# Branch A's norm factors spread through memory and multiplied on GpSimd; token sums converted in three buffers

## The chip, the cores and the metric

The kernel runs on one core of one Trainium2 chip. The metric is the time of one execution on the device in microseconds, the median of several runs. A core has five engines with an instruction queue each: TensorE (PE in the profile, with its weight loads as PEld), VectorE (DVE), ScalarE (ACT), GpSimd (POOL) and SyncE (SP), which here issues nearly all DMAs. Each engine runs its queue in order, and waits on semaphores for what other engines or DMAs must have done first.

## The reference, cut to what matters

A bidirectional encoder block in float32: 16 meta tokens and 1024 tokens of width 1024. The tokens are normed and projected; branch A (differential attention, 4 heads of 128 values, no window) and branch B (windowed attention, 8 heads) run side by side; each branch is projected and gated by a sigmoid; the sum goes through the output projection, and a SwiGLU layer and a final norm follow. The part that the change touches is the norm of branch A's heads:

```python
attn = jax.nn.softmax(s1, axis=-1) - lam * jax.nn.softmax(s2, axis=-1)
y = jnp.einsum('bhqk,bkhe->bqhe', attn, v)
...
y = rms_norm(y, subln_g) * (1.0 - lambda_init)   # per token and head, over the 128 values
...
merged = jax.nn.sigmoid(ga) * (y_a @ w_ba) + jax.nn.sigmoid(gb) * (y_b @ w_bb)
```

## The kernel before

Every float32 product is made from a high and a low part of each operand (`split`, L124: ScalarE writes the high part at L125, another engine the low part at L126), so one product is three matmuls. The gates, the projections behind the branches and the feed-forward layer use a scheme with seven products of half-size blocks in place of eight, whose operands are sums and differences of blocks.

The program runs in four stretches: norm, transposes and first projections (to about 95 us in the profile); branch B's attention with the projections of branch A (95 to 285); branch A's attention with the two gates' projections (285 to 600); the rest (600 to 1400).

**Branch B.** `attend_b` makes, for each of two groups and eight tiles of queries, scores (L417), exponentials on ScalarE (L423, with the small sink term `bes` at L425), a denominator on VectorE (L426, L427), transposes on TensorE (bpt, L458) that VectorE or ScalarE copies to SBUF (btr, L461 and L462), and products with the values (bpy). Between these stand projection matmuls (L237). Order: a scheduler with a model of the engines places the instructions of this stretch. In the same stretch `tokens_mixed` (L338 to L367) forms the sums and differences of token blocks on GpSimd that the gates' products need later. Each is split by `kept` into a tile `tst`, high part on ScalarE (L125), low part on GpSimd (L126), and stored by SyncE into `t_d`. Two buffers of the pool `kvpool` (tags q1 and q0) take turns: a split waits until the store from two splits earlier has landed.

**Branch A.** 32 tiles of queries (head h = 0 to 3, tile t = 0 to 7), one after the other. TensorE's order is written by hand: for each tile a string of `SLOTS` is read letter by letter; `s` is a step of the tile's scores (`aps`, L1054), `t` a step of transposes of the tile before (`apt`, L1084), `g` a quarter of a gate's operand group, 12 matmuls with one weight operand `wopg` (L943), `n` a step of the tail (products with the values, L1097, and the norm, `normed_a`). Heads 0 and 1 take two strings in turn, heads 2 and 3 a third one and, for every fourth tile, `SLOTS_3`. GpSimd makes the gate operands (L820 to L840: sums of weight blocks, a cast `wopg` L839, the low part L840), copies far parts of the bias mask (L1006, `far_copy`), zeroes ends of value tiles (L1026) and takes the power −1/2 (L1116). Its order here is left to the scheduler, with some ordering edges: `queue_behind(late, first)` (L373) puts an instruction behind another one in the schedule without a semaphore. SyncE loads gate weights (`wg`, L799), keys, values and token sums (`hT`, from `t_d`, L869) and stores results.

**The norm** (`normed_a`, once for each of eight groups of four tiles, (h, c) with c = 0 or 1). Head outputs stand transposed: 128 values on partitions, 512 tokens along the row. ScalarE writes the squares into `ysq` and the values times the gain into `yg`; four small matmuls with a column of ones (L1110) give the sums of squares with tokens on partitions, four columns of 128; VectorE and GpSimd turn them into the factors `f` (tile `af`, 128×4; L1114 to L1116). `N_WAIT` = 3 tail steps later four transposes of `f`, each column broadcast to 128 columns, give in a PSUM bank (`apf`, L1121) each token's factor on all 128 partitions; VectorE multiplies `yg` by that bank (L1122), and SyncE stores `yg` into `ya_d` (L1123).

Of the kernel before, what the change touches and what calls it, by code (L numbers as in the profile page):

```python
# [9 lines left out]
F32 = mybir.dt.float32  # L10
F32R = mybir.dt.float32r
# [8 lines left out]
P = 128  # L20
# [23 lines left out]
FAR_LATE = 6  # L44
LAST_B = ("T1", 4), (5, "V0"), (5, "T2"), ("T2", 6), (7, "V1"), (7, "V2")
SLOTS_LAST = "ggggntgntnt"
SLOTS_3 = "ssgsgngsstsgntgnt"
S_BUFS = (2, 2)
AT_BUFS = 2
G_BUFS = 3  # L50
# [29 lines left out]
def encoder_block(ctx: ExitStack, tc: tile.TileContext, x, meta, norm_mix, w_in, lq1, lk1, lq2, lk2,  # L80
# [254 lines left out]

    HALF = (slice(0, 512), slice(512, S))

    def tokens_mixed():  # L338
# [659 lines left out]
    s0s = [apool.tile([P, 9 * P], F32, name=f"as0_{i}") for i in range(2)]  # L998
    apool.tile([P, 9, 2, 256], F32R, tag="at", name="at_room", bufs=AT_BUFS)

    def far_copy(n):
        if n < AH * NT:
            with ExitStack() as after:
                if n > 2:
                    after.enter_context(tc.issue_after(made_g[-1].ins))
                nc.gpsimd.tensor_copy(far_m[n % 3][:, 0:S - 704], dist[:, 1600 - n % NT * P:1600 - n % NT * P + S - 704])  # L1006

    for i in range(3):
        nc.gpsimd.memset(far_m[i][:, S - 704:], 0.0)
# [25 lines left out]
    sum_a = {}  # L1035

    def scores_a(h, t, ld, s):
        slope = 2.0 ** -(2 * (h + 1))
# [62 lines left out]
    def normed_a(h, c, py):  # L1101
        nm = f"{h}_{c}"
        ysq = gwork.tile([P, 512], F32, tag="ysq", name=f"ysq_{nm}", bufs=1)
        nc.scalar.activation(ysq, py, AF.Square)
        yg = ustage.tile([P, 512], F32, tag="yg", name=f"yg_{nm}", bufs=2)
        nc.scalar.activation(yg, py, AF.Copy, scale=gsub)
        yield
        pst = bank(psum2, "sc", f"apst_{nm}", SC)
        for i in range(4):
            nc.tensor.matmul(pst[:, i:i + 1], ysq[:, i * P:(i + 1) * P], ones, start=True, stop=True)  # L1110
        f = small.tile([P, 4], F32, tag="af", name=f"af_{nm}", bufs=2)
        sums = sum_a.pop((h, c))
        e = small.tile([P, 4], F32, tag="ae", name=f"ae_{nm}", bufs=2)
        nc.vector.scalar_tensor_tensor(e, sums, EPS, sums, ALU.mult, ALU.mult)  # L1114
        nc.vector.scalar_tensor_tensor(f, pst[:, 0:4], 1.0 / P, e, ALU.mult, ALU.add)
        nc.gpsimd.tensor_tensor(f, f, neg_half, ALU.pow)  # L1116
        for _ in range(N_WAIT):
            yield
        pf = bank(psum2, "sc", f"apf_{nm}", SC)
        for i in range(4):  # L1120
            nc.tensor.transpose(pf[:, i * P:(i + 1) * P], f[:, i:i + 1].broadcast_to([P, P]), ident)  # L1121
        nc.vector.tensor_tensor(yg, yg, pf, ALU.mult)  # L1122
        nc.sync.dma_start(ya_d[h][:, c * 512:c * 512 + 512], yg)  # L1123
        yield

# [37 lines left out]
    for n in range(AH * NT + T_LAG):  # L1163
        scoring, turning = iter(()), iter(())
        if n == 1:
            fill(2)
        if n < AH * NT:
            h, t = divmod(n, NT)
            if t == 0:
                assert h < 2 or n_kept[0] == 4  # L1170
                with ExitStack() as first:
                    if not h:
                        first.enter_context(tc.high_priority())
                    ld = load_a(h)
                    load_v(h, ld[2])
                if not h:
                    ensure_g(4)
                fill(G_HEAD if h else G_FIRST)
                if not h:
                    ensure_g(N_PRE)  # L1180
                    with tc.issue_after(made_g[min(5, len(made_g) - 1)].ins):
                        for i in range(2):
                            nc.gpsimd.memset(s0s[i][:, L + 2 * NM:], 0.0)
                if not h:
                    for after, late in LAST_B:
                        behind = quarters[after][1] if isinstance(after, int) else last_unit["TV".index(after[0]) + 2 * int(after[1])][-1]
                        queue_behind([quarters[late][0]] if isinstance(late, int) else last_unit["TV".index(late[0]) + 2 * int(late[1])], behind)
                if not h:
                    order_pool.__exit__(None, None, None)
            if t % 2 == 0:  # L1190
                at_ = apool.tile([P, 9, 2, 256], F32R, tag="at", name=f"at{h}_{t}", bufs=AT_BUFS)
            s = [None, None]
            tiles.append((h, t, s, at_, ld[2]))
            scoring = scores_a(h, t, ld, s)
        if n >= T_LAG:
            turning = turn(tiles[n - T_LAG])
        for what in (SLOTS_3 if n % 4 == 3 and n >= 2 * NT else SLOTS[n % 2 if n < 2 * NT else 2]) if n < AH * NT else SLOTS_LAST:
            if what == "s":
                next(scoring, None)
            elif what == "t":  # L1200
                next(turning, None)
            elif what == "n":
                step_tail()
            else:
                fill(1)
        for _ in scoring:
            pass
        for _ in turning:
            pass
        if n >= T_LAG and tiles[n - T_LAG][1] % 2:  # L1210
            tail.append(later(tiles[n - T_LAG]))
# [753 lines left out]
```

## Time and profile before

| | |
|---|---|
| median of 3 runs | 1408.59 us (1407.03 to 1409.55) |
| profiled execution, its own time | 1409.17 us |
| its span in the profile | 1407.4 us |
| granted TensorE clock, mean | 0.999 |
| busy: TensorE, VectorE, ScalarE, GpSimd | 1395.9, 921.3, 680.0, 658.8 us |
| TensorE matmul instructions | 7171 |
| moved by DMA | 227.75 MB |

The profile comes from one execution. A busy time is the sum over an engine's instructions; matmuls overlap in the pipeline, so what a few of them cost in time is read from the distance between their starts. "Idle before, releaser" is time in which an engine stood before an instruction, and what ended it.

### The profile page before, as it was taken

What the parts mean: (1) busy time and instruction counts of PE and PEld (TensorE: products, weight loads), DVE (VectorE), ACT (ScalarE), POOL (GpSimd) and SP (SyncE); (2) the same over time, 40 slices, a digit from 0 to 9 for tenths busy, and PEclk for the clock granted to TensorE, in tenths of its full rate; (3) what the DMA queues carried; (4) which work ended last, traced back from release to release, by engine and by line L of the source; (5) the groups of instructions that cost most, each with busy time, mean ns of one, the idle gap of its engine ahead of it and who ended that gap; (6) DMA issues with size and microseconds to landing.
All of it is one profiled execution on the core that took longest, in us unless ns stands there. A gap on an engine that the chain in (4) does not pass through costs nothing.

```text
span 1407.4 us, 20700 instructions
## 1 busy us (share of the span) xinstructions
PE 1395.9 (99%) x7171; PEld 1200.2 (85%) x7171; DVE 921.3 (65%) x1587; ACT 680.0 (48%) x1317; POOL 658.8 (47%) x634
## 2 busy tenths in 40 slices
PE   9999999999999999999999999999999999999998
PEld 8989899888888989888888888888888888888886
DVE  6556676666677878657968966544455443887566
ACT  6255565555454655554446644333333333444444
POOL 4256885575786767623404054544554441000442
PEclk9999999999999999999999999999999999999999
DMA  8445658464896363495603634333223333954444
GB/s 232 91 129 172 195 181 274 140 220 119 293 307 210 115 211 106 147 311 171 210 30 130 177 114 144 125 112 112 98 98 112 105 98 101 367 183 142 119 127 146
DMA packets 193018, 227.75 MB, mean 162 GB/s; under 512 B 16952, under 2 KB 126464, under 8 KB 192784
## 3 DMA queue, kind: packets, MB, share of 16 engines
q1 hardware_dynamic: 190160, 222.80, 49.5%
q10 hardware_dynamic: 2752, 3.61, 0.9%
q8 instruction: 57, 0.93, 0.3%
q14 instruction: 49, 0.40, 0.1%
HBM read 152.48 MB, written 68.39 MB: 157 GB/s over the span
## 4 chain that ended last, share of the span: by engine, by line
PE 92%; DMA 3%; DVE 1%; issue 1%; ACT 1%; SPq 1%; POOL 0%; ACTq 0%; DVEq 0%; POOLq 0%
PE pg L1728 30%; PE pd L1832 14%; PE pg L943 12%; PE ppa L753 6%; PE aps L1054 4%; PE po L1631 4%; PE apy L1097 3%; PE pp_va L237 3%; PE pp_ka L237 2%; PE apt L1084 2%; PE pp_qa L237 2%; PE pp_qb L237 2%; PE po L1639 2%; PE bps L417 1%; PE bpy L464 1%; PE bpt L458 1%
## 5 line engine op out<-in xcount | busy, mean ns | idle before, releaser
L1728 PE MATMUL pg<-t,wop 128*128 128x512 f32 x1056 | 242.5, 389 | 0.0
L1728 PEld LDWEIGHTS pg<-t,wop 128*128 128x128 f32 x1056 | 198.3, 188 | 41.0
L126 POOL TENSOR_TENSOR wop<-wf,wop 128x512 fp32r<-128x512 f32 x114 | 151.5, 1329 | 164.5 <-ACT wop L125 154.5
L1832 PE MATMUL pd<-ob,oa 128*128 128x512 f32 x924 | 209.9, 390 | 0.2 <-DVE ob L126 0.2
L1832 PEld LDWEIGHTS pd<-ob,oa 128*128 128x128 f32 x924 | 173.5, 188 | 36.6 <-DVE ob L126 0.5
L1728 PE MATMUL pg<-b,wop 128*128 128x512 f32 x792 | 183.3, 390 | 0.0
L943 PE MATMUL pg<-hT_hi,wopg 128*128 128x512 f32 x488 | 182.1, 401 | 0.0
L1728 PEld LDWEIGHTS pg<-b,wop 128*128 128x128 f32 x792 | 148.6, 188 | 30.6
L125 ACT ACTIVATE wop<-wf 128x512 fp32r<-128x512 f32 x128 | 80.8, 632 | 73.0 <-PE pg L1728 47.6
L126 POOL TENSOR_TENSOR oa<-ra,oa 128x512 fp32r<-128x512 f32 x27 | 34.9, 1294 | 169.2 <-ACT oa L125 167.8
L1065 ACT ACTIVATE as<-as,amn 128x1040 f32<-128x1040 f32 x64 | 74.6, 1166 | 79.5 <-DVE amn L1061 78.2
L943 PEld LDWEIGHTS pg<-hT_hi,wopg 128*128 128x128 f32 x488 | 91.7, 188 | 14.1
L125 ACT ACTIVATE oa<-ra 128x512 fp32r<-128x512 f32 x77 | 48.7, 632 | 108.8 <-PE pd L1832 49.9
L943 PE MATMUL pg<-hT_lo,wopg 128*128 128x512 f32 x244 | 95.9, 393 | 0.0
L1505 DVE TENSOR_TENSOR s<-wf,wf 128x512 f32<-128x512 f32 x22 | 16.0, 728 | 111.9 <-DMA wf<-in_w_ff_up_dram 70.6
L1054 PE MATMUL aps<-ak,aq 128*128 128x352 f32 (+1 forms) x384 | 86.2, 333 | 0.0
L1057 DVE CUSTOM_DVE_ANT_0 as<-aps,dist,far_a 128x704 f32<-128x704 f32 x64 | 60.4, 944 | 21.5 <-PE aps L1054 21.2
L1054 PEld LDWEIGHTS aps<-ak,aq 128*128 128x128 f32 x384 | 63.6, 189 | 6.9
L419 DVE CUSTOM_DVE_ANT_0 bs<-bps,tbx,nsink 128x432 f32<-128x432 f32 (+1 forms) x64 | 38.4, 627 | 42.4 <-PE bps L417 30.0
L429 POOL TENSOR_SCALAR bs<-bs,bdn 128x432 f32<-128x432 f32 (+1 forms) x64 | 37.0, 597 | 51.5 <-DVE bdn L427 32.1
L1755 ACT COPY p<-pg 128x512 f32<-128x512 f32 x44 | 25.8, 587 | 66.4 <-PE pg L1728 66.4
L1097 PEld LDWEIGHTS apy<-at,av 128*128 128x128 f32 x400 | 54.1, 189 | 4.1
(340 smaller groups left out, 3142.1 us busy)
## 6 DMA issues: line engine op xcount, KB each, us to landing
ra<-aop SPq DMA_DIRECT2D x77, 256.0 KB, 2.7
wf<-in_w_ff_gate_dram SPq DMA_DIRECT2D x25, 512.0 KB, 3.6
wf<-in_w_ff_up_dram SPq DMA_DIRECT2D x25, 512.0 KB, 3.6
aop<-as SPq DMA_DIRECT2D x44, 256.0 KB, 2.1
wg_s<-in_w_in_dram SPq DMA_DIRECT2D x18, 512.0 KB, 4.7
aop<-c SPq DMA_DIRECT2D x33, 256.0 KB, 2.0
ak<-ka_d SPq DMA_DIRECT2D x16, 520.0 KB, 6.6
t_d<-tst SPq DMA_DIRECT2D x16, 512.0 KB, 5.0
```

What stands on the lines that cost most here:

```text
L125: high = nc.scalar.activation(hi, src, AF.Copy)
L126: lo_eng.tensor_tensor(lo, src, f32(hi), ALU.subtract)
L237: product = nc.tensor.matmul(ps[:, :n], a[:, c, :], b[:, c, at:at + n], start=(u == 0), stop=(u == 3 * DC - 1))
L753: nc.tensor.matmul(ps, w[:, a, j, :], src(j, b, tk), start=(j == 0 and n == 0), stop=(j == 3 and n == 2))
L943: product = nc.tensor.matmul(ps, op[:, x, c, :], h[:, 4 * d + c, HALF[t]], start=(p in (1, 6, 7) and c == 0 and i == 0), stop=(p in (2, 6, ...
L1054: nc.tensor.matmul(ps[:, :n], qs[m][:, t * P:(t + 1) * P], ks[m][:, vv, k0:k0 + n], start=(vv == 0), stop=(vv == 1))
L1057: nc.vector.tensor_tensor_reduce(s[m][:, 0:2 * n].rearrange("p (a k) -> p a k", a=2), two[:, :, :n], dist[:, u0:u0 + 2 * n].rearrange("p ( ...
L1065: nc.scalar.activation(s[m][:, 0:L], s[m][:, 0:L], AF.Exp, bias=mn[:, m, 1:2], scale=-1.0, accum_out=dn[:, 1:2] if m else first_sum)
L1097: nc.tensor.matmul(py[:, cols], v[:kp, a, k, :], at_[:kp, k, b, :], start=(k == 0 and j == 0), stop=(k == 8))
L1631: nc.tensor.matmul(sets_o[p][u], oa[:, a, u * P:(u + 1) * P], ob[:, b, :], start=(p in (1, 5) and j == 0 and k == 0), stop=(p in (2, 3) an ...
L1728: nc.tensor.matmul(ps, op[:, x, c, :], b[:, y, c, :], start=(p in (1, 5) and c == 0 and n == 0), stop=(p in (4, 2, 3) and c == 3 and n == ...
L1832: nc.tensor.matmul(ps[u], oa[:, a, u * P:(u + 1) * P], ob[:, b, :], start=(p in (1, 2, 5) and j == 0 and k == 0), stop=(p in (2, 3, 4) and ...
```

## The change

Three edits.

1. In `normed_a`, for all groups but the last one (3, 1), the transposes and VectorE's product are replaced. SyncE stores the 128×4 factors into a row `f_d` in memory, 512 elements in token order, and loads that row back into all 128 partitions of the tile `ysq`, whose squares are no longer needed. Three tail steps later in the program GpSimd multiplies `yg` by `ysq`. Ordering edges, set after the loop, place the multiply behind the far-mask copy of two tiles later (in head 3 behind one of the last gate operands), and in heads 0 to 2, c = 0, the store and the load behind the last load of the next head's keys. (3, 1) stays as it was.
2. `kept` takes three buffers in turn: q1 and q0 of `kvpool`, and bys of `bpool`.
3. In heads 2 and 3 the tiles with n % 4 = 1 get a string of their own, in which one `g` stands between the second and the third `s` instead of near the end. Those with n % 4 = 3 keep `SLOTS_3`'s string.

Lines after the first edits are shifted by 1 to 19 in the changed kernel (L458 is L463 there, L820 to L840 are L825 to L845, L1116 is L1123).

```diff
-SLOTS_3 = "ssgsgngsstsgntgnt"
+SLOTS_ODD = "ssggsgnssgtsgntnt", "ssgsgngsstsgntgnt"
...
+    f_d = [dram.tile([1, S], F32, name=f"f_d{h}") for h in range(AH)]
...
             def kept(k, t):
-                st = kvpool.tile([P, 2, 512], F32R, tag=("q1", "q0")[k % 2], name=f"tst{k}_{c}")
+                n_turned[0] += 1
+                p, tag = ((kvpool, "q1"), (kvpool, "q0"), (bpool, "bys"))[n_turned[0] % 3]
+                st = p.tile([P, 2, 512], F32R, tag=tag, name=f"tst{k}_{c}", bufs=1)
                 split(st[:, 0], st[:, 1], t, nc.gpsimd)
                 nc.sync.dma_start(t_d[k][:, :, c, :], f32(st))
...
         nc.gpsimd.tensor_tensor(f, f, neg_half, ALU.pow)
-        for _ in range(N_WAIT):
-            yield
-        pf = bank(psum2, "sc", f"apf_{nm}", SC)
-        for i in range(4):
-            nc.tensor.transpose(pf[:, i * P:(i + 1) * P], f[:, i:i + 1].broadcast_to([P, P]), ident)
-        nc.vector.tensor_tensor(yg, yg, pf, ALU.mult)
+        if (h, c) == (AH - 1, 1):
...
+        else:
+            out_f = nc.sync.dma_start(f_d[h][0, c * 512:c * 512 + 512].rearrange("(i p) -> p i", p=P), f,
+                                      allow_slow_non_contiguous=True)
+            in_f = nc.sync.dma_start(ysq, f_d[h][:, c * 512:c * 512 + 512].broadcast_to([P, 512]))
+            for _ in range(N_WAIT):
+                yield
+            scaled_a[h, c] = out_f, in_f, nc.gpsimd.tensor_tensor(yg, yg, ysq, ALU.mult)
         nc.sync.dma_start(ya_d[h][:, c * 512:c * 512 + 512], yg)
...
-        for what in (SLOTS_3 if n % 4 == 3 and n >= 2 * NT else SLOTS[n % 2 if n < 2 * NT else 2]) if n < AH * NT else SLOTS_LAST:
+        for what in (SLOTS_ODD[n % 4 // 2] if n % 2 and n >= 2 * NT else SLOTS[n % 2 if n < 2 * NT else 2]) if n < AH * NT else SLOTS_LAST:
...
+    for (h, c), (out_f, in_f, scaling) in scaled_a.items():
+        if c == 0 and h < AH - 1:
+            queue_behind([out_f, in_f], keys_a[h + 1])
+        queue_behind([scaling], far_copies[h * NT + 4 * c + 10] if h < AH - 1 else made_g[-4])
```

The edits also shift what the scheduler places. TensorE in branch B, around the transposes `bpt_2_3` of the second group (`pp_ka` is a projection, `bpy` a product with values), before:

```order
L458 MATMUL bpt_2_2_2137<-ident,bs_2_1997 128x128 x4
L237 MATMUL pp_ka_768_3161<-hT_lo,wh_c_3074 128x272
L237 MATMUL pp_ka_768_3161<-hT_hi,wl_c_3075 128x272
L237 MATMUL pp_ka_768_3161<-hT_hi,wh_c_3074 128x272
L237 MATMUL pp_ka_768_3161<-hT_lo,wh_c_3074 128x272
L458 MATMUL bpt_2_3_2147<-ident,bs_2_1997 128x128 x4
L237 MATMUL pp_ka_768_3161<-hT_hi,wl_c_3075 128x272
L455 MATMUL bpy_2_2117<-btm_157,vb_154 128x512
```

and of the change:

```order
L463 MATMUL bpt_2_2_2141<-ident,bs_2_2001 128x128 x4
L238 MATMUL pp_ka_768_3165<-hT_lo,wh_c_3078 128x272
L463 MATMUL bpt_2_3_2151<-ident,bs_2_2001 128x128 x4
L460 MATMUL bpy_2_2121<-btm_161,vb_158 128x512
L469 MATMUL bpy_2_2121<-btr_2_1_2136,vb_158 128x512 x2
L238 MATMUL pp_ka_768_3165<-hT_hi,wl_c_3079 128x272
```

Three projection matmuls that stood between `bpt_2_2` and `bpt_2_3` now come behind them.

GpSimd in branch A, around the power of the second group of head 0 (`af_1`), before:

```order
L820 TENSOR_TENSOR wg_f_1_4453<-wg_f_1_4453 128x512
L821 TENSOR_TENSOR wg_f_1_4453<-wg_f_1_4453,wg_f_0_4451 128x512
L839 CAST wopg_6_4586<-wg_f_1_4453 128x512
L1116 TENSOR_TENSOR af_1_4640<-af_1_4640,neg_half 128x4
L840 TENSOR_TENSOR wopg_6_4586<-wg_f_1_4453,wopg_6_4586 128x512
L839 CAST wopg_2_4626<-wg_f_0_4451 128x512
```

and of the change:

```order
L825 TENSOR_TENSOR wg_f_1_4454<-wg_f_1_4454 128x512
L826 TENSOR_TENSOR wg_f_1_4454<-wg_f_1_4454,wg_f_0_4452 128x512
L1123 TENSOR_TENSOR af_1_4641<-af_1_4641,neg_half 128x4
L844 CAST wopg_6_4587<-wg_f_1_4454 128x512
L845 TENSOR_TENSOR wopg_6_4587<-wg_f_1_4454,wopg_6_4587 128x512
L844 CAST wopg_2_4627<-wg_f_0_4452 128x512
```

The power, which stood between the two halves of `wopg_6`, now stands ahead of both.

SyncE at the same place, before:

```order
L869 DMA hT_lo<-t_d_92 128x2x512
L869 DMA hT_hi<-t_d_92 128x2x512
L869 DMA hT_lo<-t_d_92 128x2x512
L869 DMA hT_hi<-t_d_92 128x2x512
L869 DMA hT_lo<-t_d_93 128x512
L799 DMA wg_s_1_4690<-in_w_in_dram 128x8x128
L869 DMA hT_hi<-t_d_93 128x512 x2
L869 DMA hT_lo<-t_d_93 128x512 x2
```

and of the change:

```order
L874 DMA hT_lo<-t_d_92 128x2x512
L874 DMA hT_hi<-t_d_92 128x2x512
L1132 DMA f_d_105<-af_1_4641 128x4x1
L874 DMA hT_lo<-t_d_92 128x2x512
L874 DMA hT_hi<-t_d_92 128x2x512
L874 DMA hT_lo<-t_d_93 128x512
L1134 DMA ysq_1_4597<-f_d_105 128x512
L804 DMA wg_s_1_4693<-in_w_in_dram 128x8x128
L874 DMA hT_hi<-t_d_93 128x512 x2
L874 DMA hT_lo<-t_d_93 128x512 x2
```

The store of the factors and the load that reads it stand among the loads of token sums for the next gate half, ahead of five of them and of a load of gate weights.

More of the change, by code (lines that the diff above doesn't have):

```diff
@@ L336, in encoder_block @@
     HALF = (slice(0, 512), slice(512, S))
+    n_turned = [0]
     def tokens_mixed():
@@ L999, in encoder_block @@
     apool.tile([P, 9, 2, 256], F32R, tag="at", name="at_room", bufs=AT_BUFS)
+    far_copies = {}
     def far_copy(n):
@@ L1005, in far_copy @@
                     after.enter_context(tc.issue_after(made_g[-1].ins))
-                nc.gpsimd.tensor_copy(far_m[n % 3][:, 0:S - 704], dist[:, 1600 - n % NT * P:1600 - n % NT * P + S - 704])
+                far_copies[n] = nc.gpsimd.tensor_copy(far_m[n % 3][:, 0:S - 704], dist[:, 1600 - n % NT * P:1600 - n % NT * P + S - 704])
     for i in range(3):
@@ L1033, in load_v @@
             values_in.append(nc.sync.dma_start(f32(va)[2 * NM:3 * NM, 0, 8, :], va_d[h][:NM, 1, 8, :]))
-    sum_a = {}
+    sum_a, scaled_a = {}, {}
     def scores_a(h, t, ld, s):
@@ L1116, in normed_a @@
         nc.gpsimd.tensor_tensor(f, f, neg_half, ALU.pow)
-        for _ in range(N_WAIT):
-            yield
-        pf = bank(psum2, "sc", f"apf_{nm}", SC)
-        for i in range(4):
-            nc.tensor.transpose(pf[:, i * P:(i + 1) * P], f[:, i:i + 1].broadcast_to([P, P]), ident)
-        nc.vector.tensor_tensor(yg, yg, pf, ALU.mult)
+        if (h, c) == (AH - 1, 1):
+            for _ in range(N_WAIT):
+                yield
+            pf = bank(psum2, "sc", f"apf_{nm}", SC)
+            for i in range(4):
+                nc.tensor.transpose(pf[:, i * P:(i + 1) * P], f[:, i:i + 1].broadcast_to([P, P]), ident)
+            nc.vector.tensor_tensor(yg, yg, pf, ALU.mult)
+        else:
+            out_f = nc.sync.dma_start(f_d[h][0, c * 512:c * 512 + 512].rearrange("(i p) -> p i", p=P), f,
+                                      allow_slow_non_contiguous=True)
+            in_f = nc.sync.dma_start(ysq, f_d[h][:, c * 512:c * 512 + 512].broadcast_to([P, 512]))
+            for _ in range(N_WAIT):
+                yield
+            scaled_a[h, c] = out_f, in_f, nc.gpsimd.tensor_tensor(yg, yg, ysq, ALU.mult)
         nc.sync.dma_start(ya_d[h][:, c * 512:c * 512 + 512], yg)
```

## Prediction

> **What bounds the kernel now.** I read the page's shares and chain first, then the stretches of the program, then TensorE's waits.
>
> ```profile
> span 1407.4 us, 20700 instructions
> ...
> PE 1395.9 (99%) x7171; PEld 1200.2 (85%) x7171; DVE 921.3 (65%) x1587; ACT 680.0 (48%) x1317; POOL 658.8 (47%) x634
> ...
> PE 92%; DMA 3%; DVE 1%; issue 1%; ACT 1%; SPq 1%; POOL 0%; ACTq 0%; DVEq 0%; POOLq 0%
> ```
>
> TensorE is busy 99% of the span and 92% of the chain. A step taken from TensorE shortens the run by its own length, unless TensorE then stands still. GpSimd (POOL), at 47%, has room on average; whether it has room at the right moments has to be read place by place. The stretches (us; busy time and count of PE, PEld, DVE, ACT, POOL; granted clock; DMA share; GB/s):
>
> ```profile
> 95.00:285.00 190.00, 188.55 (x1130) 174.24 (x1129) 125.29 (x300) 108.63 (x259) 127.72 (x138) 1.00 0.62 191
> 333.00:600.00 267.00, 267.00 (x1612) 238.71 (x1611) 196.19 (x431) 145.22 (x282) 185.69 (x176) 1.00 0.60 195
> 380.00:410.00 30.00, 30.00 (x177) 26.66 (x176) 22.57 (x52) 16.30 (x33) 26.66 (x26) 1.00 0.94 327
> ```
>
> In branch A's attention (333 to 600) TensorE never stops, so nothing can be gained there but work taken from it, and any lateness of another engine would be new. In branch B's stretch (95 to 285) it stands still for 190.00 − 188.55 = 1.45 us, nearly all of it in one wait:
>
> ```profile
> PE bpt L458 <- DVE btr L462: 1.3, 1, 1.3
> ```
>
> The granted clock is 1.00 in all three, so no gain or loss of clock enters the sum.
>
> **Part 1: the transposes that go.** The rows of tile apf, and TensorE around the first group:
>
> ```profile
> L1121 PE MATMUL apf<-ident,af x32: 271/272/277, 352.0 to 591.1; 128*128 128x128 f32 x32
> L1122 DVE TENSOR_TENSOR yg<-yg,apf x8: 677/683/692, 352.6 to 591.8; 128x512 f32<-128x512 f32 x8
> ...
> 352.00 0.60 PE L1121 MATMUL apf<-ident,af 128*128 128x128 f32 x4
> 352.43 0.60 PE L1084 MATMUL apt<-ident,as 128*128 128x128 f32 x4
> ```
>
> Matmuls overlap, so the price is the distance of the starts: four transposes cost 352.43 − 352.00 = 0.43 us. Seven of the eight groups go: 7 × 0.43 = −3.0 us, all of it on the path. DVE's seven multiplies (0.68 us each) lie beside TensorE and count for nothing. The change of the slot string only moves gate steps; it adds and removes no matmul, and I price it at nothing (if the third score step then finds its bank not free, a few tenths come back; the range holds that).
>
> **Part 2: three buffers for tst.** Is the one wait of TensorE in branch B due to the buffers? Followed back through the timeline (start, length, engine, line; idle before it and who ended it):
>
> ```profile
> 224.44 0.19 ACT L423 ACTIVATION_READ_ACCUMULATOR bs<-bs,bmn 128x1 f32 x1
> 225.55 0.63 ACT L125 ACTIVATE tst<-tmix 128x512 fp32r<-128x512 f32 x1 [0.93 <-DMA t_d<-tst]
> 226.09 0.19 ACT L425 ACTIVATE bes<-bes 128x4 f32<-128x4 f32 x1
> 226.31 1.24 DVE L426 TENSOR_TENSOR bdn<-bdn,bes 128x4 f32<-128x4 f32 x1 [0.86 <-ACT bes L425]
> 227.80 0.69 DVE L462 TENSOR_TENSOR btr<-bpt,btr 128x512 fp32r<-128x512 f32 x1
> 228.55 0.65 PE L458 MATMUL bpt<-ident,bs 128*128 128x128 f32 x4 [1.25 <-DVE btr L462]
> ...
> ACT tst L125 <- DMA t_d<-tst: 13.7, 5, 4.0
> ```
>
> ScalarE stands before L125, because tst's buffer is still being stored; behind it in ScalarE's queue is the small exponential bes, behind that DVE's L426 and L462, and L462 frees the bank that TensorE wants. With a third buffer bes could start at 224.44 + 0.19 = 224.63 instead of 226.09, 1.46 us sooner, and the bank would be free at about 227.1. TensorE came to that point at 228.55 − 1.25 = 227.30. In the new order, though, it comes there three projection matmuls earlier (the order of the two kernels differs at bpt_2_3), and these start about 0.12 us apart:
>
> ```profile
> 226.88 0.28 PE L237 MATMUL pp_ka<-hT_hi,wh_c 128*128 128x272 f32 x1
> 227.00 0.29 PE L237 MATMUL pp_ka<-hT_lo,wh_c 128*128 128x272 f32 x1
> ```
>
> So it comes at about 226.93, and 0.16 us of the wait stays: −1.25 + 0.16 = −1.1 us. The bounds: −1.45 (all the standing time of the stretch) and 0 or a little above (the scheduler shuffles this stretch, and the same wait turns up at another tile).
>
> **Part 3: seven multiplies on GpSimd.** A 128×512 product of two SBUF operands on GpSimd, its waits, and its work around the second power (L1116) of head 0:
>
> ```profile
> L840 POOL TENSOR_TENSOR wopg<-wg_s,wopg x27: 1283/1294/2409, 399.7 to 593.6; 128x512 fp32r<-128x512 f32 x27
> ...
> L1116 POOL TENSOR_TENSOR af<-af,neg_half 128x4 f32<-128x4 f32 x8 | 9.2, 1154 | 35.1 <-DVE af L1115 35.1
> L1026 POOL MEMSET av<- 128x128 f32 x3 | 0.6, 204 | 18.9 <-PE apy L1097 18.9
> ...
> 384.54 0.61 POOL L839 CAST wopg<-wg_f 128x512 fp32r<-128x512 f32 x1
> 387.67 2.08 POOL L1116 TENSOR_TENSOR af<-af,neg_half 128x4 f32<-128x4 f32 x1 [2.52 <-DVE af L1115]
> 389.72 1.29 POOL L840 TENSOR_TENSOR wopg<-wg_f,wopg 128x512 fp32r<-128x512 f32 x1
> ...
> 391.27 0.63 PE L943 MATMUL pg<-hT_hi,wopg 128*128 128x512 f32 x2
> ```
>
> The multiplies add 7 × 1.29 = 9.1 us to GpSimd. It already stands 35.1 + 18.9 = 54 us before two kinds of instruction in this stretch, waiting for sums and for TensorE, and a multiply ahead of such a wait is absorbed by it. I laid the new GpSimd order over these durations and waits and compared each gate operand's completion with TensorE's first use of it. Two places are close.
>
> At 389.72 the low part of wopg_6 ends at 391.01; TensorE needs it at 391.27, the first L943 with that part: 0.26 us to spare. In the new order the cast (0.61) stands behind the power instead of ahead of it. The power waits for DVE as before, so the low part ends about 0.61 + 0.06 us later: 0.67 − 0.26 = 0.4 us late. TensorE's order passes nothing else there: **+0.4 us**.
>
> The other place is the end of branch A, where the last power and two wbhb products now stand ahead of wopg_3:
>
> ```profile
> 589.01 1.02 POOL L1116 TENSOR_TENSOR af<-af,neg_half 128x4 f32<-128x4 f32 x1 [1.43 <-DVE af L1115]
> 590.00 1.29 POOL L126 TENSOR_TENSOR wbhb<-m,wbhb 128x512 fp32r<-128x512 f32 x1
> ...
> 596.42 0.62 PE L943 MATMUL pg<-hT_hi,wopg 128*128 128x512 f32 x2
> ```
>
> From 589.01: power 1.02, two products 2.58, one of wg_s 1.29, cast 0.61, low part 1.29, together 6.8: 595.8 against the use at 596.42. 0.6 us to spare: nothing. If the power takes 2.08 as at 387.67 and one product 2.41 (the longest above), it is 1.06 + 1.12 − 0.6 = 1.6 us late, which is the upper bound. Everywhere else at least 1.9 us is left.
>
> The Trainium skill ("GPSIMD Engine Reference", section 4.1 Engine selection) speaks against the move: elementwise work on two inputs belongs on VectorE, and GpSimd takes about twice as long. The rows agree, 1.29 us against 0.68. Taken as deciding, the rule would give rival D's time; the rows speak for a cost only where GpSimd has no wait to hide it.
>
> **Part 4: two DMAs per group on SyncE.** A store of 512 four-byte elements, and a load of 256 KB that waits for it at the head of SyncE's queue. The tight place is the second group of head 0, where DMA is at 0.94 (row 380 to 410): there the token loads of the next gate half (hT, L869) stand behind it.
>
> ```profile
> DMA to landing us min/median/max: 2.2/2.2/2.2
> ...
> 391.46 0.39 SPq L869 DMA_DIRECT2D hT_lo<-t_d  x1
> 391.94 0.47 SPq L799 DMA_DIRECT2D wg_s<-in_w_in_dram  x1
> 392.50 2.31 SPq L869 DMA_DIRECT2D hT_hi<-t_d  x2
> ...
> DMA to landing us min/median/max: 5.4/7.2/9.8
> ...
> 410.38 0.39 PE L943 MATMUL pg<-hT_hi,wopg 128*128 128x512 f32 x1
> ```
>
> The first row is gsub's load (L643, 128 four-byte elements, quiet queue), the second landing row is hT_hi's between 385 and 425. The store can issue at about 389.5, when the power is done. Estimated as a transfer of its neighbourhood it lands 5.4 to 7.2 us later, near 396; till then SyncE issues nothing beyond hT_lo at 391.46, but the loads already queued are still moving: that one lands about 7 us after its issue, near 398.6. The DMA engines do not run dry, and what is lost is the added 0.26 MB at 327 GB/s, 0.8 us. The loads behind it (in all 2.3 MB with the new one, 7.1 us at that rate, and some 2 us of latency) would land 9.1 us after the store at the latest, 405; the last hT tile is needed at 410.38. I price it at nothing; the cover is 5 us, and without it each us counts in full.
>
> On the store, the Trainium skill ("DMA: Bandwidth & Descriptors", Rules for kernel authors) says that a non-contiguous last dimension becomes one descriptor per element, and advises a contiguous one. No run of before shows such a store; what it could do is the first rival.
>
> **Sum.** −3.0 − 1.1 + 0.4 = −3.7 us. On the profiled execution's own 1409.17 us (span 1407.4) that gives 1405.5; it is 0.58 above the median of the runs, 1408.59, so the forecast for the median is **1404.9**. The measurement can tell 0.2%, 2.8 us, from no change: faster is below 1405.8, slower above 1411.4.
>
> **Rivals.**
> *A. The scattered store is slow, and SyncE's queue stands behind it (slower).* If 512 elements cost four times gsub's 2.2 us behind a queue of 9.8, the store lands at 389.5 + 18.6 = 408.1, the last hT tile at 417.2, and TensorE waits 6.8 us at 410.38: 1411.7, and more if its other places stall too. It decides from the point where the store takes longer than 410.38 − 9.1 − 389.5 = 11.8 us. Against it: 512 elements spread over 16 engines. Chance 0.12.
> *B. Branch B's wait only moves.* ScalarE is freed, but another bank is late in the shuffled order: −3.0 + 0.4 = −2.6, 1406.0. The same time would come if the buffers were not the cause, that is, if the change did not do what it says there. For it: the wait stays within 0.16 us of showing even in my sum. Chance 0.2.
> *C. GpSimd is late at the end of branch A.* −3.0 − 1.1 + 0.4 + 1.6 = −2.1, 1406.5. Chance 0.1.
> *D. GpSimd becomes the bound of the stretch*: its far-mask copies and gate operands slip by what the multiplies add, at worst 9.1 us: 1404.9 + 9.1 = 1414. Against it are the 54 us of waits and 185.69 busy us in 267. Chance 0.04.
>
> **How the numbers follow.** The forecast has 0.54. Its bounds are −3.0 − 1.45 = −4.45 (1404.1 for the median) and B and C together, −3.0 + 0.4 + 1.6 = −1.0 (1407.6). Runs of one kernel lay 1.56 below and 0.96 above their median, so the range is 1402.5 to 1408.6. It leaves out A and D, 0.16. Faster: nearly all of the forecast, 0.48, and a third of B and C, 0.09: 0.57. Slower: A and D for the most part, 0.14. The rest, 0.29, is no difference.
>
> **What would show it.** Right: TensorE's instructions fall by 28; no wait of bpt for btr above 0.2 us in branch B and no wait of ScalarE for t_d worth naming; one wait of pg for wopg near 391, about 0.4 us; TensorE otherwise busy from 333 to 600; the f_d stores land within 8 us. Wrong: a wait of pg for hT near 407 to 411 (A), bpt waiting again (B), pg waiting for wopg near 593 (C) or at many places (D), or the stretch from 333 to 600 shorter by clearly less than 3 us with no wait at all, which would mean that the transposes were not on the path.

## The result and the profile after

The changed kernel is slower: 1421.86 us (median of 5 runs, 1420.71 to 1426.20) against 1407.03 us of the kernel before in the same comparison, a ratio of 1.011 with a 95% interval of 1.0089 to 1.0131. (The 1408.59 us of the table above is the median of the first three of the same five runs of before.) The forecast was 1404.9 us with a range of 1402.5 to 1408.6. The profiled execution took 1426.2 us and is the longest of the five, so the losses read from it are somewhat larger than those of the median. Its page:

```profile
span 1424.4 us, 20686 instructions
...
PE 1398.3 (98%) x7143; PEld 1198.9 (84%) x7143; DVE 918.0 (64%) x1580; ACT 681.7 (48%) x1317; POOL 667.0 (47%) x641
...
PE 87%; DMA 6%; POOL 2%; issue 2%; SPq 1%; DVE 1%; ACT 0%; ACTq 0%; DVEq 0%; POOLq 0%
```

The 28 transposes are gone, and the chain now holds 6% of DMA and 2% of GpSimd. The stretches show where TensorE stands (columns as before):

```profile
95.00:285.00 190.00, 189.78 (x1139) 176.07 (x1138) 122.09 (x305) 111.86 (x261) 129.41 (x139) 1.00 0.63 193
333.00:600.00 267.00, 254.56 (x1505) 225.05 (x1504) 183.18 (x409) 133.01 (x263) 175.09 (x169) 0.99 0.69 182
600.00:640.00 40.00, 37.37 (x167) 29.78 (x166) 22.37 (x30) 19.81 (x33) 21.27 (x17) 1.00 0.88 298
```

Branch B stands still for 0.2 us in place of 1.45. Branch A, where TensorE never stopped, now stands for 12.4 us before 600 and 2.6 behind it. What it waits for between 280 and 640:

```profile
PE aps L1061 <- DMA ak<-ka_d: 5.1, 3, 3.9
PE pg L948 <- POOL wopg L844: 3.3, 1, 3.3
PE pg L948 <- DMA hT_hi<-t_d: 2.9, 3, 1.7
PE pg L948 <- POOL wopg L845: 2.0, 3, 1.1
PE apf L1129 <- POOL af L1123: 1.5, 1, 1.5
```

These are late loads (keys `ak`, token sums `hT`) and late work of GpSimd, and GpSimd itself stood for a load. The first group of head 0 shows how. SyncE's queue, then GpSimd's, then TensorE's:

```profile
353.07 0.44 SPq L1132 DMA_DIRECT2D f_d<-af  x1
353.61 0.94 SPq L804 DMA_DIRECT2D wg_f<-in_w_in_dram  x1
...
357.54 1.57 SPq L911 DMA_DIRECT2D g_d<-g  x1
368.45 0.33 SPq L1134 DMA_DIRECT2D ysq<-f_d  x1
```

```profile
368.91 1.27 POOL L825 TENSOR_TENSOR wg_f<-wg_f 128x512 f32<-128x512 f32 x1 [9.33 <-DMA wg_f<-in_w_in_dram]
```

```profile
372.25 0.50 PE L948 MATMUL pg<-hT_hi,wopg 128*128 128x512 f32 x1 [3.29 <-POOL wopg L844]
```

The store issues at 353.07, and the load that waits for it comes out of SyncE's queue at 368.45, 15.4 us later. But the gate weights wg_f, issued behind the store at 353.61 and waiting for nothing, also took until 368.9, when GpSimd gets them. So more than SyncE's queue was late. The DMA engines over that time, in the kernel before (first row) and in the changed one (the rest):

```profile
357.50:368.40 10.90, 10.90 (x65) 9.71 (x64) 4.49 (x12) 3.89 (x7) 6.97 (x8) 1.00 1.00 327
```

```profile
357.50:368.40 10.90, 9.87 (x60) 8.66 (x59) 5.33 (x13) 3.86 (x7) 1.91 (x2) 1.00 1.39 99
368.40:380.00 11.60, 7.69 (x34) 6.12 (x33) 3.27 (x9) 2.55 (x5) 10.64 (x11) 0.85 0.96 272
374.00:376.00 2.00, 2.00 (x7) 1.72 (x6) 0.58 (x2) 0.47 (x1) 1.92 (x4) 0.50 0.74 216
376.00:378.00 2.00, 2.00 (x11) 1.72 (x10) 0.16 (x1) 0.78 (x2) 2.00 (x2) 0.67 0.92 289
```

They are busy (a share of 1.39, more than one packet counted at a time) and move 99 GB/s in place of 327, with a store of only 2 KB among what they carry. Part of the gap is that SyncE, standing, issued less; the experiments below separate the two. The last three rows show a second loss: TensorE stood for 3.29 and 0.62 us before 373.6, and its granted clock was 0.50 from 374 to 376 and 0.67 from 376 to 378.

TensorE did not wait behind every store. The waits above lie behind the first (4.9 us, 362 to 374), the second (3.1 us for token sums, 414 to 420) and the third (3.9 us for keys, at 458.6), and at the end of branch A (2.6 us for GpSimd, 605 to 613); 0.3 us at 396.7 is the wait for wopg_6 that the prediction priced at 0.4.

### The profile page after: what moved, and what is told of

Same layout as the page of the kernel before. It is cut to its first block, busy times and chain, and to the rows that moved or that the text cites. A ratio compares the mean times of both kernels' runs of the same rounds, so it can differ in the third digit from the quotient of the medians.

```text
span 1424.4 us, 20686 instructions
## 1 busy us (share of the span) xinstructions
PE 1398.3 (98%) x7143; PEld 1198.9 (84%) x7143; DVE 918.0 (64%) x1580; ACT 681.7 (48%) x1317; POOL 667.0 (47%) x641
## 4 chain that ended last, share of the span: by engine, by line
PE 87%; DMA 6%; POOL 2%; issue 2%; SPq 1%; DVE 1%; ACT 0%; ACTq 0%; DVEq 0%; POOLq 0%
PE pg L1747 29%; PE pd L1851 15%; PE pg L948 7%; PE ppa L758 6%; PE po L1650 4%; PE pp_ka L238 3%; PE pp_va L238 3%; PE aps L1061 3%; PE pp_qb L238 2%; PE apy L1104 2%; PE bps L422 2%; DMA ak<-ka_d 2%; PE pp_qa L238 2%; PE po L1658 2%; PE apt L1091 2%
## 5 line engine op out<-in xcount | busy, mean ns | idle before, releaser
L1094 ACT ACTIVATE at<-apt 128x512 fp32r<-128x512 f32 (+1 forms) x96 | 46.3, 487 | 29.5 <-PE apt L1091 28.8
```

The costliest lines, as they stand in the source:

```text
L1094: nc.scalar.activation(hi, pt[:kp, :nb], AF.Copy)
```

## Experiments

Times are medians; the ratio is to the kernel before on the same chip, and is not exactly the quotient of the two medians. A packet is one contiguous piece that a DMA writes.

### What in the norm factors' way costs the time

Four kernels change the store and what hangs on it, or leave it out. The rest of the program is that of the changed kernel.

**rows16**: the store in 128 rows of 16 bytes, undone by a stepped read in the multiply.

```diff
-            out_f = nc.sync.dma_start(f_d[h][0, c * 512:c * 512 + 512].rearrange("(i p) -> p i", p=P), f, ...
+            out_f = nc.sync.dma_start(f_d[h][0, c * 512:c * 512 + 512].rearrange("(p i) -> p i", p=P), f)
...
-            scaled_a[h, c] = out_f, in_f, nc.gpsimd.tensor_tensor(yg, yg, ysq, ALU.mult)
+            scaled_a[h, c] = out_f, in_f, nc.gpsimd.tensor_tensor(
+                yg.rearrange("q (i p) -> q i p", p=P), yg.rearrange("q (i p) -> q i p", p=P),
+                ysq.rearrange("q (p i) -> q i p", p=P), ALU.mult)
```

> Edit: the factors are stored as 128 rows of 16 bytes (token order within a row of memory changes), and GpSimd's multiply reads the loaded tile with a step of four to undo it. SyncE's order, the wait of the load for the store and the bytes stay the same; only the number of packets falls from 512 to 128 per store. Theory P (packets: the many four-byte packets hold all DMA engines, about 10 us per store, and everything queued behind them is late): the store lands in a quarter of the extra time, some 4 to 7 us after its issue, and the kernel comes near the forecast, 1404 to 1408 us. Rival Q (queue: SyncE stands at the load until the store has landed, and a write to memory followed by a read takes that long whatever its packets): no change, 1418 to 1423. Rival G (GpSimd's 9.1 us of multiplies and its new order are what delay TensorE): no change either, or slower if the stepped read costs GpSimd more than 1.3 us.

**unread**: the scattered store goes where nobody reads; the load takes a row that one packet has written before.

```diff
+            row_f = nc.sync.dma_start(f_d[h][:, c * 512:c * 512 + 512], ysq[0:1, :])
-            out_f = nc.sync.dma_start(f_d[h][0, c * 512:c * 512 + 512].rearrange("(i p) -> p i", p=P), f, ...
+            out_f = nc.sync.dma_start(f_e[h][0, c * 512:c * 512 + 512].rearrange("(i p) -> p i", p=P), f, ...
```

> Leaves out the right factors: the 512-packet store goes to a row that nobody reads, and the load reads a row of 2 KB that one packet has written, from the squares, some microseconds earlier. So SyncE no longer waits for the scattered store, but the store still goes through the DMA engines. Theory P: still slow, 1414 to 1422, and loads issued shortly after the scattered store take 10 us or more. Rival Q: 1404 to 1408. Rival G: 1418 to 1423.

**one_row**: only that row, no scattered store.

```diff
-            out_f = nc.sync.dma_start(f_d[h][0, c * 512:c * 512 + 512].rearrange("(i p) -> p i", p=P), f, ...
+            out_f = nc.sync.dma_start(f_d[h][:, c * 512:c * 512 + 512], ysq[0:1, :])
```

> Leaves out the right factors: in place of the scattered store one row of 2 KB (the first partition of the squares) is stored, and loaded to all partitions as in the change. One packet instead of 512, the same load that waits for its store, the same GpSimd multiplies. Theory P: 1403 to 1407. Rival Q: 1412 to 1422, since the load still waits for a store at the head of SyncE's queue. Rival G: 1418 to 1423.

**no_dma**: neither store nor load.

```diff
-            out_f = nc.sync.dma_start(f_d[h][0, ...
-            in_f = nc.sync.dma_start(ysq, f_d[h][:, c * 512:c * 512 + 512].broadcast_to([P, 512]))
...
```

> Leaves out the right factors and both DMAs: GpSimd multiplies by the squares as they stand in the tile. What is left of the first edit are the transposes that are gone and the seven multiplies on GpSimd. Theories P and Q: 1402.5 to 1405.5, my forecast without any cost of DMA. Rival G: 1412 or more.

| kernel | median, us | ratio (95% interval) |
|---|---|---|
| before | 1405.97 | |
| rows16 | 1406.39 | 1.0005 (0.9996 to 1.0013) |
| unread | 1424.28 | 1.0133 (1.0118 to 1.0147) |
| one_row | 1405.46 | 0.9998 (0.9990 to 1.0007) |
| no_dma | 1405.32 | 1.0000 (0.9991 to 1.0008) |

The rival of SyncE's queue falls. In the changed kernel SyncE stood 63.5 us in all for the seven stores; in unread it waits for none of them (only 6.1 us for the rows that one packet writes), and the kernel is the slowest of all. So does that of GpSimd: with the same multiplies in no_dma there is no loss. The store itself costs the time. The waits of TensorE show what is late (unread, 280 to 640):

```profile
PE aps L1062 <- DMA ak<-ka_d: 7.8, 1, 7.8
PE pg L949 <- POOL wopg L845: 3.1, 1, 3.1
PE pg L949 <- DMA hT_hi<-t_d: 2.5, 2, 1.6
```

When is it late? The first store of unread is issued at 351.02. The DMA engines in unread from 4 us behind that on, and in no_dma (no store at all) over the second of the two stretches:

```profile
355.00:357.00 2.00, 2.00 (x12) 1.78 (x11) 1.21 (x3) 0.56 (x1) 1.33 (x2) 1.00 0.91 303
357.00:366.00 9.00, 8.92 (x55) 7.68 (x53) 4.92 (x12) 3.91 (x8) 1.66 (x2) 1.00 1.04 139
```

```profile
357.00:366.00 9.00, 9.00 (x56) 8.09 (x55) 4.78 (x11) 3.86 (x7) 7.88 (x8) 1.00 0.87 272
```

In the packet records of unread's trace the small writes of this store begin between 355 and 357 and are noted at 9 ns each. The throughput falls behind them, to 139 GB/s for 9 us, and it is packets of other transfers that then take long: 73 of them over 0.5 us, up to 3.4, where no_dma has one. So the tiny packets do not fill the engines while they pass; the transfers behind them are slow. For what those wait the trace does not say.

And a surprise: with neither store nor load the kernel is not below before. That comes further down.

### Number, size, or neighbours

Three stores take the place of the scattered one in unread; all stay unread, and the load is the same. In the last two the stores also stand elsewhere: the first goes out at 7.9 us (pk512x64) or 7.7 us (pk512x512), and the other six in pairs (in pk512x64 at 351.8 and 359.1, 434.0 and 442.2, 502.5 and 511.8).

```diff
 pk128x4 (one column of the factors, side by side)
+            out_f = nc.sync.dma_start(f_e[h][0, c * 128:c * 128 + 128].rearrange("(p i) -> p i", p=P), f[:, 0:1])
 pk512x64, r = 16 (and pk512x512, r = 128, the tile read four times)
+            with tc.issue_after(power.ins):
+                out_f = nc.sync.dma_start(f_e[h][0, 0:512 * r].rearrange("(i p r) -> p i r", p=P, r=r),
+                                          ident[:, 0:64].rearrange("p (i r) -> p i r", r=r))
```

> As the run whose scattered store nobody reads, but that store holds one column of the factors only: 128 packets of 4 bytes in place of 512. (Leaves out the right factors, as there.) If a store's cost goes with the number of its packets, a quarter of the cost of 512, most of it covered, as with 128 packets of 16 bytes: 1405.5 to 1409. If there is a fixed cost of a store of tiny pieces whatever their number: near 1424.

> The unread store again in 512 packets, of 64 bytes each, from a constant tile. If the number of packets is what costs: 1420 to 1428, as with 512 packets of 4 bytes. If their size is what costs (tiny pieces of memory written): clearly less, under 1415.

> The unread store in 512 packets of 512 bytes, 256 KB in all. If the number of packets is what costs, whatever their size: 1422 or more, with the bytes on top. If small pieces are dear and large ones are not: the 0.26 MB at some 330 GB/s, 0.8 us of DMA time for each of seven stores, mostly covered: 1405.5 to 1409.

pk128x4 took 1414.89 us (1.0063, 1.0050 to 1.0076), pk512x64 1405.36 (0.9992, 0.9983 to 1.0001), pk512x512 1419.61 (1.0095, 1.0080 to 1.0110), before 1407.12 (23 runs, one of them of 8040.86 us). A quarter of the packets costs half as much as all of them, and four times as many, of 64 bytes, cost nothing: the count of packets (theory P of the expectations) falls. pk512x512 fits neither of its expectations, but it does not speak for packets either: from its first score to its last gate product it takes what pk512x64 takes,

```profile
L1062 PE MATMUL aps<-ak,aq x384: 309/322/431, 292.1 to 584.2; 128*128 128x352 f32 x128, 128*128 128x336 f32 x64
L949 PE MATMUL pg<-hT_hi,wopg x488: 387/394/500, 273.1 to 612.5; 128*128 128x512 f32 x163
```

612.5 − 292.1 = 320.4 us against 597.9 − 278.2 = 319.7; it is 14 us late when branch A begins. In branch B its TensorE waits for VectorE and GpSimd, 9.4 us in four waits that pk512x64 has not. The store at 7.7 us, which is 256 KB there, stands between the first loads of x; whether it is the cause was not tried.

Size or neighbours is left. **apart64** and **apart512** are unread again, with the store in unread's place and with elements 64 and 512 bytes apart.

```diff
-            out_f = nc.sync.dma_start(f_e[h][0, c * 512:c * 512 + 512].rearrange("(i p) -> p i", p=P), f, ...
+            out_f = nc.sync.dma_start(
+                f_e[h][0, c * 512 * r:c * 512 * r + 512 * r].rearrange("(i p r) -> p i r", p=P, r=r)[:, :, 0:1],
+                f.rearrange("p (i r) -> p i r", r=1), allow_slow_non_contiguous=True)   # r = 16, 128
```

> The unread scattered store again, 512 packets of 4 bytes in the same order on SyncE, but each element 64 bytes apart from the next in memory. (Leaves out the right factors, as there.) If a packet of 4 bytes is dear by itself: 1422 to 1426, as when they lie side by side. If they are dear because neighbours go to the same piece of memory (64 packets of 64 bytes a partition-row cost nothing, 128 packets of 4 bytes side by side landed as late as 512): 1405 to 1408, and the store lands some 6 us after its issue in place of 12.

> The same with 512 bytes between neighbours. If neighbours in a piece of 64 bytes get in each other's way: as with 64 bytes between them. If the piece is larger than 64 bytes: this one is faster than that one, near 1405 to 1408. If 4 bytes are dear by themselves: 1422 to 1426.

apart64 took 1405.10 us (0.9993, 0.9984 to 1.0002), apart512 1405.44 (0.9995, 0.9986 to 1.0004), before 1405.85. The same 512 packets of 4 bytes, 64 bytes apart, cost nothing. The landing that the profile gives for the scattered store is 12.0 us behind its issue in unread, 12.4 in pk128x4 and 8.2 in apart64 and apart512 (some 6 were expected). What the DMA engines move between 355 and 365, around the landing of the first store in branch A (last column, GB/s), in unread, pk128x4, rows16, apart64, pk512x64, in this order, and in no_dma as the yardstick:

```profile
355.00:365.00 10.00, 10.00 (x62) 9.03 (x61) 5.13 (x13) 4.42 (x8) 2.00 (x3) 1.00 1.04 172
```

```profile
355.00:365.00 10.00, 10.00 (x61) 8.97 (x60) 4.65 (x13) 4.08 (x7) 1.99 (x3) 1.00 1.07 211
```

```profile
355.00:365.00 10.00, 10.00 (x61) 8.83 (x59) 4.51 (x12) 3.90 (x7) 6.06 (x6) 1.00 1.10 286
```

```profile
355.00:365.00 10.00, 10.00 (x62) 9.03 (x61) 5.27 (x13) 4.28 (x8) 6.82 (x7) 1.00 0.97 308
```

```profile
355.00:365.00 10.00, 10.00 (x62) 8.96 (x60) 4.51 (x12) 3.91 (x7) 6.13 (x6) 1.00 1.09 345
```

```profile
355.00:365.00 10.00, 10.00 (x62) 9.00 (x61) 4.74 (x13) 4.17 (x8) 7.49 (x8) 1.00 0.93 305
```

With no store it is 305 (371 in the kernel before, whose loads come at other times). Sixteen writes to each 64 bytes (the first two): 172 and 211. Four (rows16): 286. One (apart64, pk512x64): 308 and 345, not below no store at all. And it is so at every store: over the 8 us from 2 us behind each issue unread moves 236, 213, 239, 39, 291, 55 and 47 GB/s, apart64 354, 370, 341, 101, 379, 100 and 66. So small writes that lie closer together than 64 bytes get in each other's way, and while they do the DMA engines move less and what is queued behind is late. How large the piece is within which they collide stays open: counted per 256 bytes the writes are 64, 16 and 4, in the same order. Nor was a distance of 32 bytes tried.

The Trainium skill ("DMA: Bandwidth & Descriptors", section Specifications) says that below 512 bytes a DMA does read-modify-write. Small size alone does not cost here, as apart64 and pk512x64 show, both of packets below 512 bytes. A read-modify-write of one piece by many writers would fit all the rows of the stores, but no run shows it as such.

### The other two edits, and the first one alone

**tst3** is before with the second edit, **slots** with the third, **norm16** with the first in rows of 16 bytes.

> The second edit alone: three buffers for tst, all else as before. My forecast's term: TensorE's wait of 1.25 us in branch B goes, -1.1 us, 1404.9 against 1406.0. Rival V: that wait was a matter of the one profiled execution (1409.2 us, at the slow end of the runs of before, whose median over 29 runs is 1406.0), so the median hardly holds it: within 0.4 us of before.

> The third edit alone: the new string for tiles with n % 4 = 1 in heads 2 and 3. My forecast: no change, 1405.5 to 1406.5. Rival: the third score step of these tiles finds its bank still being read, some tenths in each of four tiles, +0.5 to +1.5 us.

> The first edit alone, with the store in 16-byte rows; two buffers for tst and the old strings. TensorE's order is that of before without the seven groups of transposes. If the transposes were worth 3.0 us and GpSimd's new order costs the 0.5 us near 388 and 1.2 us at the end of branch A that the profile of the 16-byte kernel shows: 1406.0 - 3.0 + 1.7 = 1404.7. If the gain is eaten by something that the first edit does not hold (the shuffle of branch B, the strings): 1403.0 to 1403.8.

tst3 1405.84 us (0.9997, 0.9988 to 1.0006), slots 1405.52 (0.9998, 0.9989 to 1.0006), norm16 1406.70 (1.0004, 0.9995 to 1.0012), before 1406.16. None differs from before, and norm16 misses its expectation of 1404.7. For norm16 the waits of TensorE between 280 and 640 say why; its order there is that of before without the seven groups of transposes:

```profile
PE pg L946 <- POOL wopg L843: 1.3, 2, 1.0
PE aps L1059 <- DVE amn L1062: 0.4, 2, 0.2
PE aps L1059 <- DMA ak<-ka_d: 0.2, 1, 0.2
```

These are five waits, at 387.7, 419.4, 429.3, 511.3 and 592.8, that before does not have. Each costs more than the time that TensorE stands, since the starts of the matmuls around it also lie further apart than usual. Measured from the last start at the usual distance to the first one that is at the usual distance again, against the same matmuls in before, they cost 0.56, 0.56, 0.56, 0.49 and 1.34 us: 3.5 us. For the first, before and norm16:

```profile
391.03 0.40 PE L943 MATMUL pg<-hT_lo,wopg 128*128 128x512 f32 x1
...
392.21 0.60 PE L1084 MATMUL apt<-ident,as 128*128 128x128 f32 x4
```

```profile
386.95 0.40 PE L946 MATMUL pg<-hT_lo,wopg 128*128 128x512 f32 x1
387.65 0.73 PE L946 MATMUL pg<-hT_hi,wopg 128*128 128x512 f32 x2 [0.30 <-POOL wopg L843]
...
388.69 0.60 PE L1089 MATMUL apt<-ident,as 128*128 128x128 f32 x4
```

That is 1.74 us against 1.18. The five together take all of the 3.0 us: from the first score to the last gate product TensorE needs 320.1 us in norm16 (277.7 to 597.8) and 319.8 in before (281.4 to 601.2). The first and the last wait, 1.9 us, are GpSimd's order. The other three, 1.6 us, are for score banks and keys; that the transposes used to give time for these is argued and not shown, since tst3, which has all its transposes, also shows one wait of 0.2 us for a score bank.

### GpSimd's order mended

**norm16_ordered** and **norm16_eased** add ordering edges to norm16 for the two waits for wopg; **norm16_two_places** also holds ScalarE's order, and **norm16_two_places_tst3** has the three buffers too.

```diff
 norm16_ordered
+    queue_behind([powers[0, 1]], made_g[25])
+    queue_behind([powers[AH - 1, 1]], made_g[61])
+    queue_behind(first_lows, powers[AH - 1, 1])
 norm16_eased: the second edge instead, and one on ScalarE
+    queue_behind([powers[AH - 1, 1]], subs_g[-1])
+    queue_behind(yb_highs[-4:], q_copies[-1])
 norm16_two_places: also, for the first two sigmoids of the gates
+        if len(gate_ops) < 3:
+            queue_behind([gate_ops[-1]], q_copies[-1])
```

> As the run with the first edit alone, and three ordering edges on GpSimd: the power of group (0, 1) behind both parts of wopg_6, the power of (3, 1) behind both parts of wopg_3, and the two wbhb products behind that power. If the two waits of TensorE for wopg are what GpSimd's order costs, they go, and the whole of the transposes comes out: 1402.7 to 1403.5. If they were covered by something else late at the same places (a bank, a load): no better than the run without the edges.

> The first edit alone in 16-byte rows, with edges that leave ScalarE's copy of the q bank where it was: the power of (0, 1) behind wopg_6, the last subtraction for wopg_3 ahead of the power of (3, 1), the wbhb products behind that power, and the second half of branch B's splits on ScalarE behind the copy of q. If GpSimd's order is what took the gain back near 388 and at the end of branch A, some 1.2 of the 1.7 us come back: 1404.7 to 1405.5 against 1406.1 of before. If new waits come up in their place: 1406 or more.

> The first edit alone in 16-byte rows, with GpSimd's order changed at the two late places only (the power of (0, 1) behind wopg_6, the last subtraction for wopg_3 ahead of the power of (3, 1)), and ScalarE's order at the end of branch A held as it is without these edges. If GpSimd's order is what takes the gain back there: the waits of pg for wopg go and the time falls by 1.2 to 1.7 us against the kernel without edges, 1.0 to 1.5 us below before. If the time is set otherwise: within 0.5 us of before.

> As the run with the two places mended, and the three buffers for tst. If the wait of TensorE in branch B comes in some executions only and the third buffer keeps it away: 0 to 0.6 us below that run, and no wait of bpt for btr in the profile; 1.2 to 2.0 us below before. If three buffers cost elsewhere: above that run.

norm16_ordered took 1411.61 us (1.0035, 1.0021 to 1.0048; before 1406.16), norm16_eased 1408.37 (1.0016, 1.0007 to 1.0025; before 1407.12). The waits for wopg are gone, but with these edges ScalarE's copy of the q bank came later, and TensorE waits for it (4.3 us in norm16_ordered, 3.1 in norm16_eased). In norm16_ordered:

```profile
PE pg L948 <- ACT q L977: 4.3, 1, 4.3
```

With the copy held in its place norm16_two_places took 1404.71 us (0.9995, 0.9986 to 1.0004) and norm16_two_places_tst3 1404.14 (0.9988, 0.9980 to 0.9997; before 1405.85). That is 0.12% below before, and the only interval that lies wholly below 1; with so many kernels tried, one such interval could also come by chance. Its waits between 280 and 640:

```profile
PE aps L1064 <- DMA ak<-ka_d: 0.6, 1, 0.6
PE aps L1064 <- DVE amn L1067: 0.5, 2, 0.3
```

No wopg any more; keys and a score bank are still late.

## Why the prediction was wrong, step by step

**The failed step: the price of the store (part 4).** I took the landing of a transfer in the neighbourhood, 5.4 to 7.2 us, and said that the loads already queued keep moving meanwhile, so that the DMA engines do not run dry, and priced the store at nothing. The stores of the changed kernel, as far as the profile gives their landing:

```profile
DMA to landing us min/median/max: 10.1/10.6/13.9
```

By SyncE's queue the seven took 9.5 to 15.6 us, the first 15.4. At the place where I had looked, the second group of head 0, it was 10.7 us (394.95 to 405.62). That is under the 11.8 us that I named as the turning point, and TensorE still waited there for token sums, 3.1 us between 414 and 420. So the landing was not the whole of the failed step: the queued loads did not keep moving (in the 8 us from 2 us behind this store unread moved 213 GB/s, apart64 370). Rival A, with a chance of 0.12, had the sign and the shape (a store of tiny elements is slow), but its mechanism was half of it: it let SyncE's queue stand and the DMA engines work. Its store of 18.6 us was longer than any measured, and its 1411.7 us was still 10 us too low. In unread SyncE waited for none of the scattered stores and the loss was 18 us: what was lost were the DMA engines, whose throughput was lower behind all seven stores. A shape of transfer that the profile of before does not show, 512 neighbouring elements written one by one, was bounded by a load of 128 elements on a quiet queue; it would have had to be priced far more widely.

**Part 1, the transposes, −3.0 us.** The price holds: in norm16 the matmuls behind each group of transposes come some 0.4 us sooner against those of before, but its five new waits use up 3.5 us. What failed is that nothing else was to cost: part 3 priced GpSimd's order at 0.4 us where it took 1.9, and three waits for score banks and keys, 1.6 us, stand in no part.

**Part 3, GpSimd.** The mechanism and its places were right. At the first I expected 0.4 us; in norm16 the wait was 0.30, 0.56 with its aftermath. At the end of branch A I priced nothing with a bound of 1.6; it took 1.03, 1.34 with its aftermath (the wait is 0.8 in one_row and no_dma, whose multiplies have no stepped read). Rival C's wait was the case, not the exception: I had added six durations of one execution and found 0.6 us to spare, less than the spread of a single one of them (the power alone: 1.02 and 2.08 in the rows shown). Rival D did not come: with 9.1 us more on GpSimd, no_dma stands at a ratio of 1.0000. The rule of the Trainium skill ("GPSIMD Engine Reference", section 4.1 Engine selection) holds for the duration, 1.29 us against 0.68, and did not decide the time.

**Part 2, three buffers, −1.1 us.** The wait of bpt for btr comes in some executions: of the six profiled kernels with two buffers before, norm16_ordered and norm16_two_places show it, slots, norm16 and norm16_eased don't. None of the twelve with three buffers does, which fits that the third buffer ends it. But the three executions that show it are long ones for their kernels: 1409.17 us against medians of before of 1405.85 to 1407.12, 1414.86 against 1411.61, 1408.31 against 1404.71. I had made the sum against an execution at the upper end of its runs, and then carried the term over to the median, which does not hold it. tst3 shows what is left: 0.9997 (0.9988 to 1.0006).

**The slot string** was priced at nothing, and slots shows no difference (0.9998, 0.9989 to 1.0006).

So even with a store that costs nothing, the three edits are worth nothing that shows, and not −3.7: one_row and no_dma are at 0.9998 and 1.0000, with intervals of about 0.0008 (1.2 us) to either side.

## What to carry to other kernels

Before a tiny transfer is put down as "some latency", ask how its pieces lie in memory: behind 512 writes of 4 bytes side by side this kernel's DMA engines moved half as much for some 9 us (139 against 272 GB/s), while the same writes 64 bytes apart, or rows of 16 bytes with the order undone by a stepped read, cost little or nothing. When a step is taken off an engine that never stops, look at what arrives just in time for the steps behind it: here the 3.0 us came back as five waits of 0.2 to 1.0 us that no row of before shows. And check a wait against more than one execution before a term of a sum rests on it.

## What the runs showed of the hardware

- Neighbouring small writes: seven stores of 512 writes of 4 bytes side by side cost the kernel 18 us (unread), the same writes 64 bytes apart nothing (apart64). Over 355 to 365 the DMA engines moved 172 GB/s with such a store and 305 with none (no_dma). A load queued behind such a store, with which it has nothing to do, landed 15 us after its issue (wg_f in the changed kernel, 353.61 to 368.9).
- A GpSimd multiply that reads one operand with a step of four elements took 1.56 us in place of 1.29 (medians of rows16 and one_row). The kernels' times do not tell the two apart clearly (1.0005, 0.9996 to 1.0013, beside 0.9998, 0.9990 to 1.0007).
- A short stop of TensorE costs more than the stop: in norm16 0.30 us of waiting delayed the next starts by 0.56. In the changed kernel, behind waits of 3.29 and 0.62 us, the granted clock was 0.50 from 374 to 376, 0.67 from 376 to 378 and 1.00 again from 378 to 380.
